# Embedding projections and two LayerNorms moved between the last two products of an MLP, with partial results combined one stage earlier

## The chip, the core and the metric

The kernel runs on one core of a Trainium2 chip. The metric is the device time of one execution in microseconds (us); the time before is the median of three runs. The core has a matrix engine (TensorE, PE in the profile), a vector engine (VectorE, DVE), an engine for activations and copies (ScalarE, ACT), a general one (GpSimd, POOL) and a queue that issues DMA transfers (SyncE, SP). The engines run in parallel, each through its own instructions in a fixed order, and wait for each other by semaphores.

## The reference, cut to what matters

Two layers over 512 tokens with a width of 1024. The token mixers (an mLSTM in layer 0, windowed attention in layer 1) are not touched by the change. The end of each layer is:

```python
for i in range(DEPTH):                      # 2 layers
    ...                                     # token mixer -> mix
    x = layer_norm(DEEPNORM_ALPHA * x + mix, mix_ln_g[i], mix_ln_b[i])
    x = layer_norm(DEEPNORM_ALPHA * x + squared_relu_mlp(x, mlp_w_up[i], mlp_w_down[i]), mlp_ln_g[i], mlp_ln_b[i])
    x = x + jax.nn.sigmoid(x @ ple_w_gate[i] + ple_b_gate[i]) * (p[i] @ ple_w_proj[i])

def squared_relu_mlp(x, w_up, w_down):      # 1024 -> 4096 -> 1024
    return jnp.square(jax.nn.relu(x @ w_up)) @ w_down
```

`p[i]` is the per-layer embedding, 512 x 256. The product `p[i] @ ple_w_proj[i]` needs nothing of x; the gate product `x @ ple_w_gate[i]` needs the x of the second LayerNorm.

## The kernel before, in words

All products run in float32 split into a high and a low part: `split` lets ACT cast the raw tile (L76, 128x1024) to the high part and DVE subtract it (L77) for the low part, and `mm3` issues three matmuls (high-high, high-low, low-high: L88, L89, L90). Weights arrive through SP's queue in a ring of three `raw` buffers and are split into rings of six `whi` and six `wlo` buffers; a DMA waits until its raw buffer has been split, a cast until the products that read its `whi` buffer are done.

The residual stream x lies in four tiles `res[0..3]` of 128 tokens x 1024. For the products it is transposed on PE (`transpose_in`, L129, eight 128x128 blocks for a tile, in two PSUM banks of the tag `tp`, of which there are three) and written to XH by ACT (L133) and to XL by DVE (L134).

`mlp` handles the 4096 hidden columns in four quarters q. Each quarter has an up-projection (eight weight tiles, `wstat`, with relu, square and the operand sums of a Strassen-like scheme in `evac`) and then a down-projection by seven products instead of eight, called in `seven`: A11 (step M1), A12 (M2), S1 (M5), S2 (M6), S4 (M3), S3 (M7), A22 (M4). Each product has 2 x 4 k-blocks x 3 = 24 matmuls of 128x512 and two results (a = 0, 1), each in a PSUM bank (tag `mm`, five banks). `on(step, a, bank)` adds a result into the residual tiles and into the gathered partial sums T1 (M1), T6 (M6) and T7 (M7), half a tile (128x512) at a time on DVE. In quarters 0 to 2 T1, T6 and T7 are only gathered; in the last quarter they are combined and added to the residual, `bn_stats` is taken of each finished half, and `ln_finish` normalises a tile: two full-tile DVE steps (L145, L146, with the power -0.5 on POOL, L138, between) and `transpose_in`. Tiles 0 and 1 are finished in step M3 or behind it, tiles 2 and 3 in step M4. S23 and S4A in the profile are the operands of S2 and S3, and of S4 and A22.

Then `ple` loads and splits the embedding (`ph`, `pl`) and the projection weights, computes the projections (2 halves x 4 tiles x 2 k-blocks x 3 = 48 matmuls of 128x512) and copies them to `pj` tiles on ACT (L684), and then computes the gate product, 2 halves x 4 tiles x 24 matmuls, each followed by bias, sigmoid, multiply and add.

The order on each engine is not the order of the code: a scheduler reorders by priority and data dependence when the kernel is built, and the order is then fixed.

Of the kernel before, what the change touches and what calls it, by code (L numbers as in the profile page):

```python
# [45 lines left out]
def yoco_kernel(ctx: ExitStack, tc: tile.TileContext, A: dict, out: bass.AP):  # L46
# [3 lines left out]
    def pool(name, bufs=1, stack=ctx, **kw):  # L50
        return stack.enter_context(tc.tile_pool(name=name, bufs=bufs, **kw))
# [19 lines left out]
    def f32(t):  # L71
        return t.bitcast(F32)
# [36 lines left out]
    def tsl(t):  # L109
        return slice(t * P, (t + 1) * P)  # L110
# [29 lines left out]
    def ln_finish(t, st, g, b, mlp_next=True):  # L140
        mv = small.tile([P, 2], F32, tag="mv", name="mv")
        V.bn_aggr(mv, st)
# [3 lines left out]
        V.scalar_tensor_tensor(res[t], res[t], rs, b, ALU.mult, ALU.add)  # L146
# [339 lines left out]

    sp = {}

    def seven(A_, wsrc, on):

        w0, w1 = wsrc(0), wsrc(1)
        r11, r21 = two((w0, 0, True)), two((w0, 2, False))
        r12, r22 = two((w1, 0, True)), two((w1, 2, True))

        def ops(raw):
            out = []
            for c in range(2):
# [56 lines left out]
    def mlp(i, side):  # L554
# [6 lines left out]
        for q in range(NQ):  # L561
# [31 lines left out]
            if q == 0:  # L593
                j0 = 4
                w = [load_w(A["w_up"][i, j], 1024) for j in range(j0)]
                ps = [mm_bank() for _ in range(j0)]
                for a in (0, 256):
                    for j in range(j0):
                        wh, wl = w[j]
                        for k in range(KD):  # L600
                            sl = slice(k * P, (k + 1) * P)
                            mm3(ps[j][:, a:a + 256], wh[:, sl], wl[:, sl], XH[:, k, a:a + 256], XL[:, k, a:a + 256], k == 0, k == KD - 1)
                        evac(ps[j], j, a, a + 256)
            for j in range(j0, 8):
                wstat(A["w_up"][i, 8 * q + j], lambda ps: evac(ps, j, 0, S))
            last = q == NQ - 1
            lo_, hi_ = slice(0, 512), slice(512, 1024)
            gb_ = []

            def gather(acc, bank):  # L610
                if q == 0:
                    ACT.copy(acc, bank)
                else:
                    V.tensor_add(acc, acc, bank)

            def on(step, a, bank):
                r0, r1 = res[a], res[2 + a]
                t1, t6, t7 = T1[:, a, :], T6[:, a, :], T7[:, a, :]
                if step == "M1":
                    gather(t1, bank)  # L620
                    if last:
                        V.tensor_add(r0[:, lo_], r0[:, lo_], t1)
                elif step == "M2":
                    V.tensor_add(r0[:, lo_], r0[:, lo_], bank)
                    if last:
                        V.bn_stats(sts[a][:, 0, :], r0[:, lo_])
                        if a == 1:
                            for x, n in ("h", "mlp_ln_g"), ("l", "mlp_ln_b"):
                                v = pm.tile([P, 4, 256], F32R, tag=f"A11{x}", name=f"A11{x}")
                                v = f32(v).rearrange("p k c -> p (k c)")  # L630
                                nc.gpsimd.dma_start(v, A[n][i].partition_broadcast(P))  # L631
                                gb_.append(v)
                elif step == "M5":
                    V.tensor_add(r1[:, hi_], r1[:, hi_], bank)
                    if last:
                        V.tensor_add(r0[:, hi_], r0[:, hi_], r1[:, hi_])
                elif step == "M6":
                    gather(t6, bank)
                    if last:
                        V.tensor_sub(t6, t6, t1)  # L640
                        V.tensor_add(r0[:, hi_], r0[:, hi_], t6)
                elif step == "M7":
                    gather(t7, bank)
                    if last:
                        V.tensor_add(t7, t7, t6)
                        V.tensor_add(r1[:, hi_], r1[:, hi_], t7)
                        V.tensor_sub(r1[:, lo_], r1[:, lo_], t7)
                        V.bn_stats(sts[2 + a][:, 1, :], r1[:, hi_])
                elif step == "M3":
                    V.tensor_add(r0[:, hi_], r0[:, hi_], bank)  # L650
                    if last:
                        V.bn_stats(sts[a][:, 1, :], r0[:, hi_])
                        ln_finish(a, sts[a], *gb_, mlp_next=False)
                elif step == "M4":
                    V.tensor_add(r1[:, lo_], r1[:, lo_], bank)
                    if last:
                        V.bn_stats(sts[2 + a][:, 0, :], r1[:, lo_])
# [3 lines left out]
            seven(sset((at(A11), at(A12))), lambda half: [A["w_down"][i, half, 4 * q + c] for c in range(4)], on)  # L661
        mctx.close()

    def ple(i, last, side):
        plctx = ExitStack()
        pp = pool(f"pp{i}", stack=plctx, side=side, reuse_waits="tile")
        ph = pp.tile([P, 2, S], F32R, name="ph")
        pl = pp.tile([P, 2, S], F32R, name="pl")
        raw = wpool.tile([P, 1024], F32, tag="raw", name="wraw", bufs=3)
        nc.sync.dma_start(raw, A["pT"][i])  # L670
        split(raw, 1024, flat(ph), flat(pl))
        bg = bcast(A["ple_b_gate"][i])
        if not last:
            bo = bcast(A["b_b_o"])
        pjs = [sp["s"].tile([P, 1024], F32, tag="rb", name="pj", bufs=6) for _ in range(NT)]
        for half in range(2):
            hs = slice(half * 512, (half + 1) * 512)
            wph, wpl = load_w(A["w_proj"][i, half], 1024)
            for t in range(NT):
                pj = mm_bank()  # L680
                for k in range(2):
                    sl = slice(k * 512, (k + 1) * 512)
                    mm3(pj, ph[:, k, tsl(t)], pl[:, k, tsl(t)], wph[:, sl], wpl[:, sl], k == 0, k == 1)
                ACT.copy(pjs[t][:, hs], pj)  # L684
        for half in range(2):
            w = [load_w(A["w_gate"][i, half, c], 1024) for c in range(4)]
            for t in range(NT):
# [22 lines left out]
        plctx.close()  # L710
# [5 lines left out]
    ple(0, False, "right")  # L716
    c7.close()
    kctx = ExitStack()
    pk = pool("pk", stack=kctx, side="right", reuse_waits="tile")
# [209 lines left out]

    c7 = seven_pools(1, "left")  # L930
    mlp(1, "left")
    ple(1, True, "left")
    c7.close()
    pctx.close()
    mctx[0].close()
# [67 lines left out]
```

## Time and profile before

| | |
|---|---|
| time, median of 3 runs | 1261.61 us (1261.51 to 1261.62) |
| the profiled execution | 1262.99 us, its span 1261.3 us |
| mean granted PE clock | 0.972 |
| PE busy | 1196.9 us (95%) |
| DVE busy | 869.6 us (69%) |
| ACT busy | 586.7 us (47%) |
| POOL busy | 147.6 us (12%) |

The profile is one execution. Rows of the timeline give start, duration, engine, line, operation, output<-input, shape, count and, in brackets, the idle time of the engine before the row with what ended it. Matmuls overlap in the pipeline, so their rate is read from start to start. The ends of the two MLPs lie at about 552 to 597 us and 1167 to 1211 us.

### The profile page before, as it was taken

Reading aid. Unit: us, or ns where it says so; the run is one execution under the profiler, and the core shown is the slowest. Engines: PE = TensorE matmul, PEld = TensorE weight load, DVE = VectorE, ACT = ScalarE, POOL = GpSimd, SP = SyncE. Lnnn points to the kernel's source line nnn. Section 1 sums busy time; section 2 is a strip of 40 time slices with the busy share of each in tenths; the row PEclk is TensorE's granted clock in tenths of the full one; section 3 lists DMA queues with packets and bytes.
Section 4 is the critical chain, followed back from the end, with each engine's and each line's share of the span. In section 5 each row is a group of like instructions: output and inputs, shape, how many; then the busy total and the mean of one; then the engine's idle time right before and its main releaser. Section 6 shows DMA issues by size and latency. Waiting matters only on the chain.

```text
span 1261.3 us, 15669 instructions
## 1 busy us (share of the span) xinstructions
PE 1196.9 (95%) x5918; PEld 1017.4 (81%) x5918; DVE 869.6 (69%) x1429; ACT 586.7 (47%) x1010; POOL 147.6 (12%) x245
## 2 busy tenths in 40 slices
PE   8999999999999999977989898999999999999598
PEld 8899988888888888865868897789888888888386
DVE  6555567696595785996474788486848759569934
ACT  4544542664553644634233545336546346364331
POOL 1011110000000000000154663210000000000100
PEclk9999999999999999996999999989999999999799
DMA  7222224506125053132242211351350521602311
GB/s 242 90 87 68 84 76 161 198 17 192 60 93 161 14 167 101 34 121 80 84 159 67 68 35 34 127 208 34 108 159 1 184 84 65 185 18 67 117 51 50
DMA packets 35708, 124.54 MB, mean 99 GB/s; under 512 B 4065, under 2 KB 4593, under 8 KB 35633
## 3 DMA queue, kind: packets, MB, share of 16 engines
q1 hardware_dynamic: 33552, 116.46, 28.8%
q0 software_dynamic: 2080, 7.09, 1.8%
q8 instruction: 46, 0.75, 0.2%
q14 instruction: 30, 0.24, 0.1%
HBM read 119.34 MB, written 4.19 MB: 98 GB/s over the span
## 4 chain that ended last, share of the span: by engine, by line
PE 84%; DVE 10%; ACT 2%; DMA 2%; issue 2%; POOL 0%; SPq 0%; DVEq 0%; ACTq 0%
PE mm L88 26%; PE mm L89 26%; PE mm L90 26%; DVE wlo L77 1%; PE tp L129 1%; DVE res L146 1%; ACT pr L838 1%; DVE res L145 1%; DVE QS L807 1%; DVE smax L824 1%; PE tp L88 1%; DVE sc L823 1%; PE tp L89 1%; PE tp L90 1%; DMA xraw<-in_xT_dram 1%
## 5 line engine op out<-in xcount | busy, mean ns | idle before, releaser
L76 ACT CAST whi<-wraw 128x1024 fp32r<-128x1024 f32 (+1 forms) x168 | 173.6, 1037 | 257.1 <-PE mm L90 117.3
L77 DVE TENSOR_TENSOR wlo<-wraw,whi 128x1024 fp32r<-128x1024 f32 (+1 forms) x152 | 184.4, 1216 | 155.3 <-ACT whi L76 154.6
L89 PE MATMUL mm<-XL,whi 128*128 128x512 f32 (+1 forms) x640 | 236.5, 370 | 0.0
L90 PE MATMUL mm<-XH,wlo 128*128 128x512 f32 (+1 forms) x640 | 236.3, 370 | 0.0
L88 PE MATMUL mm<-XH,whi 128*128 128x512 f32 (+1 forms) x640 | 235.0, 370 | 0.2 <-ACT XH L133 0.2
L88 PE MATMUL mm<-whi,XH 128*128 128x512 f32 (+2 forms) x424 | 147.7, 349 | 7.9 <-DVE kv L769 4.1
L89 PE MATMUL mm<-wlo,XH 128*128 128x512 f32 (+2 forms) x424 | 147.6, 348 | 0.0
L90 PE MATMUL mm<-whi,XL 128*128 128x512 f32 (+2 forms) x424 | 147.3, 348 | 0.0
L90 PEld LDWEIGHTS mm<-XH,wlo 128*128 128x128 f32 x640 | 121.7, 190 | 19.9
L89 PEld LDWEIGHTS mm<-XL,whi 128*128 128x128 f32 x640 | 121.7, 190 | 19.8
L88 PEld LDWEIGHTS mm<-XH,whi 128*128 128x128 f32 x640 | 120.6, 190 | 20.3 <-ACT XH L133 0.5
L76 ACT CAST whi<-rb 128x1024 fp32r<-128x1024 f32 x80 | 84.1, 1051 | 106.5 <-PE mm L89 54.4
L77 DVE TENSOR_TENSOR wlo<-rb,whi 128x1024 fp32r<-128x1024 f32 x80 | 97.4, 1222 | 38.9 <-ACT whi L76 38.9
L88 PEld LDWEIGHTS mm<-whi,XH 128*128 128x128 f32 x424 | 82.0, 193 | 15.9 <-DVE kv L769 4.5
L89 PEld LDWEIGHTS mm<-wlo,XH 128*128 128x128 f32 x424 | 82.0, 194 | 8.2 <-issue 1.5
L90 PEld LDWEIGHTS mm<-whi,XL 128*128 128x128 f32 x424 | 82.0, 194 | 6.9 <-issue 0.8
L631 POOL DMA_DIRECT2D A11h<-in_mlp_ln_g_dram x2 | 1.2, 581 | 590.6 <-PE mm L90 590.6
L129 PE MATMUL tp<-ident,res 128*128 128x128 f32 x160 | 30.2, 339 | 35.8 <-DVE res L146 32.6
L129 PEld LDWEIGHTS tp<-ident,res 128*128 128x128 f32 x160 | 23.5, 175 | 42.4 <-issue 36.7
L89 PE MATMUL mm<-wlo,S23h 128*128 128x512 f32 x128 | 50.7, 396 | 0.0
L89 PE MATMUL mm<-wlo,S4Ah 128*128 128x512 f32 x128 | 50.6, 396 | 0.0
L88 PE MATMUL mm<-whi,S23h 128*128 128x512 f32 x128 | 50.6, 395 | 0.0
(310 smaller groups left out, 2408.7 us busy)
## 6 DMA issues: line engine op xcount, KB each, us to landing
wraw<-in_w_up_dram SPq DMA_DIRECT2D x64, 512.0 KB, 3.6
rb<-in_w_down_dram SPq DMA_DIRECT2D x48, 512.0 KB, 4.4
wraw<-in_w_down_dram SPq DMA_DIRECT2D x16, 512.0 KB, 3.9
wraw<-in_w_gate_dram SPq DMA_DIRECT2D x16, 512.0 KB, 3.6
wraw<-in_w_vo_dram SPq DMA_DIRECT2D x19, 412.0 KB, 3.3
wraw<-in_w_qk_dram SPq DMA_DIRECT2D x8, 512.0 KB, 3.9
wraw<-in_w_out_dram SPq DMA_DIRECT2D x8, 512.0 KB, 3.9
wraw<-in_w_q_dram SPq DMA_DIRECT2D x8, 512.0 KB, 4.1
```

Of the source, the lines that this page charges most:

```text
L76: ACT.copy(hi, raw)
L77: eng.tensor_sub(lo, raw, f32(hi))
L88: PE.matmul(o, lh, rh, start=start, stop=False)
L89: PE.matmul(o, lh, rl, start=False, stop=False)
L90: PE.matmul(o, ll, rh, start=False, stop=stop)
L129: PE.transpose(pt[:, tsl(j)], src[:, tsl(b + j)], ident)
L145: V.scalar_tensor_tensor(res[t], res[t], mv[:, 0:1], g, ALU.subtract, ALU.mult)
L146: V.scalar_tensor_tensor(res[t], res[t], rs, b, ALU.mult, ALU.add)
L807: V.tensor_sub(QS[other, hs, tsl(t)], pv[own], f32(QS)[own, hs, tsl(t)])
L823: V.copy_predicated(cur, mk, prev)
L824: V.tensor_reduce(smax[:, :, pr], cur, AX.X, ALU.max)
L838: ACT.activation(pt_[:, par, pr, :], scs[pr][:, par, :], AF.Exp, scale=ASCALE, bias=nm[:, par, pr:pr + 1], accum_out=sm[:, par, pr:pr + 1])
```

## The change

The embedding's load, split and projections become a function `embed`, which takes its two operand tiles from the buffers of A12 (free after product A12) where it had a memory pool of its own before. `seven` gets a callback `between`, run after the weights of the last product are split and before that product: in the last quarter it runs `embed` and then `ln_finish` for tiles 0 and 1. The combination of T1, T6 and T7 of the first three quarters goes into the fourth up-projection (14 half-tile operations per layer), so that the last quarter adds only its own results: M1 is copied by ACT, M6 and M7 are read directly out of their banks.

```diff
-    def seven(A_, wsrc, on):
+    def seven(A_, wsrc, on, between=None):
...
-        product("A22", ops(r21), "M4")
+        w = ops(r21)
+        if between:
+            between()
+        product("A22", w, "M4")
...
             for j in range(j0, 8):
                 wstat(A["w_up"][i, 8 * q + j], lambda ps: evac(ps, j, 0, S))
+                if last and j == 2:
+                    for a in range(2):
+                        r0, r1 = res[a], res[2 + a]
+                        t1, t6, t7 = T1[:, a, :], T6[:, a, :], T7[:, a, :]
+                        for op, r, x in ((V.tensor_add, r0[:, lo_], t1), (V.tensor_sub, t6, t1), (V.tensor_add, r0[:, hi_], t6),
+                                         (V.tensor_add, r0[:, hi_], r1[:, hi_]), (V.tensor_add, t7, t6),
+                                         (V.tensor_add, r1[:, hi_], t7), (V.tensor_sub, r1[:, lo_], t7)):
+                            op(r, r, x)
...
                 if step == "M1":
-                    gather(t1, bank)
                     if last:
-                        V.tensor_add(r0[:, lo_], r0[:, lo_], t1)
+                        ACT.copy(t1, bank)
+                        add(r0, lo_)
+                    else:
+                        gather(t1, bank)
...
+                elif step == "M6":
                     if last:
-                        V.tensor_add(r0[:, hi_], r0[:, hi_], r1[:, hi_])
-                elif step == "M6":
-                    gather(t6, bank)
+                        V.tensor_sub(t6, bank, t1)
+                        V.tensor_add(r0[:, hi_], r0[:, hi_], t6)
+                    else:
+                        gather(t6, bank)
+                elif step == "M7":
                     if last:
-                        V.tensor_sub(t6, t6, t1)
-                        V.tensor_add(r0[:, hi_], r0[:, hi_], t6)
-                elif step == "M7":
-                    gather(t7, bank)
-                    if last:
-                        V.tensor_add(t7, t7, t6)
+                        V.tensor_add(t7, t6, bank)
                         V.tensor_add(r1[:, hi_], r1[:, hi_], t7)
                         V.tensor_sub(r1[:, lo_], r1[:, lo_], t7)
-                        V.bn_stats(sts[2 + a][:, 1, :], r1[:, hi_])
+                        stat(2 + a, 1)
+                    else:
+                        gather(t7, bank)
                 elif step == "M3":
-                    V.tensor_add(r0[:, hi_], r0[:, hi_], bank)
-                    if last:
-                        V.bn_stats(sts[a][:, 1, :], r0[:, hi_])
-                        ln_finish(a, sts[a], *gb_, mlp_next=False)
+                    add(r0, hi_)
+                    stat(a, 1)
...
+            def between():
+                embed(i, *(pm.tile([P, 4, 256], F32R, tag=f"A12{x}", name=f"A12{x}") for x in "hl"))
+                for a in range(2):
+                    ln_finish(a, sts[a], *gb_, mlp_next=False)
```

In the new order of instructions the projections' operands carry the names A12h and A12l. On PE, at the end of product S3 in layer 0, there stood:

```order
L88 MATMUL mm<-whi,S23h 128x512
L89 MATMUL mm<-wlo,S23h 128x512
L90 MATMUL mm<-whi,S23l 128x512
L88 MATMUL mm<-whi,S4Ah 128x512
L89 MATMUL mm<-wlo,S4Ah 128x512
L90 MATMUL mm<-whi,S4Al 128x512
```

and now stand:

```order
L88 MATMUL mm<-whi,S23h 128x512
L89 MATMUL mm<-wlo,S23h 128x512
L90 MATMUL mm<-whi,S23l 128x512
L88 MATMUL mm<-whi,A12h 128x512
L89 MATMUL mm<-wlo,A12h 128x512
L90 MATMUL mm<-whi,A12l 128x512
```

All 48 projection matmuls come here, and the 24 of A22 after them. On PE, at the end of A22, there stood the transposes of all four tiles (res_1745 to res_1748 are tiles 0 to 3) and then the projections:

```order
L88 MATMUL mm<-whi,S4Ah 128x512
L89 MATMUL mm<-wlo,S4Ah 128x512
L90 MATMUL mm<-whi,S4Al 128x512
L129 MATMUL tp<-ident,res_1745 128x128 x8
L129 MATMUL tp<-ident,res_1746 128x128 x8
L129 MATMUL tp<-ident,res_1747 128x128 x8
L129 MATMUL tp<-ident,res_1748 128x128 x8
L88 MATMUL mm<-whi,ph 128x512
L89 MATMUL mm<-wlo,ph 128x512
```

and now stand those of tiles 0 and 1 and, among them, the first gate matmuls:

```order
L90 MATMUL mm<-whi,S4Al 128x512
L129 MATMUL tp<-ident,res_1745 128x128 x8
L129 MATMUL tp<-ident,res_1746 128x128 x4
L88 MATMUL mm<-whi,XH 128x512
L89 MATMUL mm<-wlo,XH 128x512
L88 MATMUL mm<-whi,XH 128x512
L89 MATMUL mm<-wlo,XH 128x512
L129 MATMUL tp<-ident,res_1746 128x128 x4
L90 MATMUL mm<-whi,XL 128x512
L88 MATMUL mm<-whi,XH 128x512
```

The transposes of tiles 2 and 3 now come after the 48 gate matmuls of tiles 0 and 1 (first half). On DVE, at the LayerNorm of the first two tiles, there stood:

```order
L145 SCALAR_TENSOR_TENSOR res_1745<-res_1745,mv,A11h 128x1024
L137 TENSOR_SCALAR rs<-mv 128x1
L145 SCALAR_TENSOR_TENSOR res_1746<-res_1746,mv,A11h 128x1024
L657 BN_STATS lst<-res_1747 128x6
L77 TENSOR_TENSOR wlo<-wraw,whi 128x1024
L648 BN_STATS lst<-res_1748 128x6
L655 TENSOR_TENSOR res_1748<-res_1748,mm 128x512
L146 SCALAR_TENSOR_TENSOR res_1745<-res_1745,rs,A11l 128x1024
L77 TENSOR_TENSOR wlo<-wraw,whi 128x1024
L146 SCALAR_TENSOR_TENSOR res_1746<-res_1746,rs,A11l 128x1024
```

and now stand (L632 adds A22's results, L134 writes the low part of the transposed tiles):

```order
L145 SCALAR_TENSOR_TENSOR res_1746<-res_1746,mv,A11h 128x1024
L146 SCALAR_TENSOR_TENSOR res_1745<-res_1745,rs,A11l 128x1024
L77 TENSOR_TENSOR wlo<-wraw,whi 128x1024
L146 SCALAR_TENSOR_TENSOR res_1746<-res_1746,rs,A11l 128x1024
L632 TENSOR_TENSOR res_1747<-res_1747,mm 128x512
L77 TENSOR_TENSOR wlo<-wraw,whi 128x1024
L632 TENSOR_TENSOR res_1748<-res_1748,mm 128x512
L636 BN_STATS lst<-res_1747 128x6
L77 TENSOR_TENSOR wlo<-wraw,whi 128x1024
L134 TENSOR_TENSOR XL<-tp,XH 128x4x128 x3
```

Both A22 additions now come after the LayerNorm of tiles 0 and 1, and two weight splits stand between them and the first low part. The 14 combining operations of each layer stand, in the order that was built, among the last products of the third quarter, between weight splits of the fourth up-projection. The order of the attention stage between the two MLPs is the same but for a few exchanged rows.

More of the change, by code (lines that the diff above doesn't have):

```diff
@@ L603, in mlp @@
                         evac(ps[j], j, a, a + 256)
+            last = q == NQ - 1
+            lo_, hi_ = slice(0, 512), slice(512, 1024)
             for j in range(j0, 8):
                 wstat(A["w_up"][i, 8 * q + j], lambda ps: evac(ps, j, 0, S))
-            last = q == NQ - 1
-            lo_, hi_ = slice(0, 512), slice(512, 1024)
+                if last and j == 2:
[6 more added lines that the diff above has]
+                            op(r, r, x)
             gb_ = []
@@ L618, in on, with add, stat @@
                 t1, t6, t7 = T1[:, a, :], T6[:, a, :], T7[:, a, :]
+                def add(r, h):
+                    V.tensor_add(r[:, h], r[:, h], bank)
+                def stat(t, half):
+                    if last:
+                        V.bn_stats(sts[t][:, half, :], res[t][:, hi_ if half else lo_])
                 if step == "M1":
-                    gather(t1, bank)
                     if last:
-                        V.tensor_add(r0[:, lo_], r0[:, lo_], t1)
+                        ACT.copy(t1, bank)
+                        add(r0, lo_)
+                    else:
+                        gather(t1, bank)
@@ L623, in on @@
                 elif step == "M2":
-                    V.tensor_add(r0[:, lo_], r0[:, lo_], bank)
-                    if last:
[L626 to L634, printed above, removed]
-                    if last:
-                        V.tensor_add(r0[:, hi_], r0[:, hi_], r1[:, hi_])
-                elif step == "M6":
-                    gather(t6, bank)
-                    if last:
-                        V.tensor_sub(t6, t6, t1)
-                        V.tensor_add(r0[:, hi_], r0[:, hi_], t6)
-                elif step == "M7":
-                    gather(t7, bank)
-                    if last:
-                        V.tensor_add(t7, t7, t6)
+                    add(r0, lo_)
@@ new lines, in on @@
+                    stat(a, 0)
+                    if last and a == 1:
+                        for x, n in ("h", "mlp_ln_g"), ("l", "mlp_ln_b"):
+                            v = pm.tile([P, 4, 256], F32R, tag=f"A11{x}", name=f"A11{x}")
+                            v = f32(v).rearrange("p k c -> p (k c)")
+                            nc.gpsimd.dma_start(v, A[n][i].partition_broadcast(P))
+                            gb_.append(v)
+                elif step == "M5":
+                    add(r1, hi_)
+                    if last:
+                        add(r0, hi_)
+                elif step == "M6":
+                    if last:
+                        V.tensor_sub(t6, bank, t1)
[3 more added lines that the diff above has]
+                elif step == "M7":
+                    if last:
+                        V.tensor_add(t7, t6, bank)
@@ L646, in on @@
                         V.tensor_add(r1[:, hi_], r1[:, hi_], t7)
                         V.tensor_sub(r1[:, lo_], r1[:, lo_], t7)
-                        V.bn_stats(sts[2 + a][:, 1, :], r1[:, hi_])
+                        stat(2 + a, 1)
+                    else:
+                        gather(t7, bank)
                 elif step == "M3":
-                    V.tensor_add(r0[:, hi_], r0[:, hi_], bank)
+                    add(r0, hi_)
+                    stat(a, 1)
+                elif step == "M4":
+                    add(r1, lo_)
@@ L651, in on @@
                     if last:
-                        V.bn_stats(sts[a][:, 1, :], r0[:, hi_])
-                        ln_finish(a, sts[a], *gb_, mlp_next=False)
-                elif step == "M4":
-                    V.tensor_add(r1[:, lo_], r1[:, lo_], bank)
-                    if last:
-                        V.bn_stats(sts[2 + a][:, 0, :], r1[:, lo_])
+                        stat(2 + a, 0)
                         ln_finish(2 + a, sts[2 + a], *gb_, mlp_next=False)
+            def between():
+                embed(i, *(pm.tile([P, 4, 256], F32R, tag=f"A12{x}", name=f"A12{x}") for x in "hl"))
+                for a in range(2):
+                    ln_finish(a, sts[a], *gb_, mlp_next=False)
@@ L660, in mlp @@
             at = lambda pair: lambda k, a: tuple(p[:, k, tsl(a)] for p in pair)
-            seven(sset((at(A11), at(A12))), lambda half: [A["w_down"][i, half, 4 * q + c] for c in range(4)], on)
+            seven(sset((at(A11), at(A12))), lambda half: [A["w_down"][i, half, 4 * q + c] for c in range(4)], on,
+                  between if last else None)
         mctx.close()
[L664 to L668, printed above, removed]
+    pjs = []
@@ L669, in ple, with embed @@
+    def embed(i, ph, pl):
         raw = wpool.tile([P, 1024], F32, tag="raw", name="wraw", bufs=3)
@@ L671, in ple @@
         split(raw, 1024, flat(ph), flat(pl))
[L672 to L675, printed above, removed]
+        ph, pl = (flat(x).rearrange("p (k s) -> p k s", k=2) for x in (ph, pl))
+        pjs[:] = [sp["s"].tile([P, 1024], F32, tag="rb", name="pj", bufs=6) for _ in range(NT)]
         for half in range(2):
@@ L684, in ple @@
                 ACT.copy(pjs[t][:, hs], pj)
+    def ple(i, last):
+        bg = bcast(A["ple_b_gate"][i])
+        if not last:
+            bo = bcast(A["b_b_o"])
         for half in range(2):
@@ L715, in yoco_kernel @@
     mlp(0, "right")
-    ple(0, False, "right")
+    ple(0, False)
     c7.close()
@@ L931, in yoco_kernel @@
     mlp(1, "left")
-    ple(1, True, "left")
+    ple(1, True)
     c7.close()
```

1 line of the change is left out of this document (removed).

## Prediction

> **What bounds the kernel now.** I read the page first, then the list of waits, then TensorE's timeline where the longest wait falls, then the other queues there.
>
> ```profile
> PE 1196.9 (95%) x5918; PEld 1017.4 (81%) x5918; DVE 869.6 (69%) x1429; ACT 586.7 (47%) x1010; POOL 147.6 (12%) x245
> ...
> PE tp L129 <- DVE res L146: 32.6, 9, 10.5
> PE sc L818 <- ACT pr L838: 4.9, 5, 2.1
> ```
>
> TensorE (PE) is busy for 95% of the span, so time can only come from work taken off it or from its waits. The second group gives total us, times and the longest: 32.6 us of waiting belong to one place, transposes (L129) that wait for VectorE's (DVE) second LayerNorm step (L146); the next wait is 4.9 us. The timeline (start, us, idle before in brackets) shows it at the end of each MLP, layer 0 first:
>
> ```profile
> 560.39 0.39 PE L90 MATMUL mm<-whi,S4Al 128*128 128x512 f32 x1
> 571.19 1.94 PE L129 MATMUL tp<-ident,res 128*128 128x128 f32 x8 [10.40 <-DVE res L146]
> 573.52 2.29 PE L129 MATMUL tp<-ident,res 128*128 128x128 f32 x8 [0.39 <-DVE mv L142]
> 578.50 1.94 PE L129 MATMUL tp<-ident,res 128*128 128x128 f32 x8 [2.69 <-DVE res L146]
> 582.28 1.94 PE L129 MATMUL tp<-ident,res 128*128 128x128 f32 x8 [1.83 <-DVE res L146]
> 583.87 0.78 PE L88 MATMUL mm<-whi,ph 128*128 128x512 f32 x1
> 584.44 0.63 PE L89 MATMUL mm<-wlo,ph 128*128 128x512 f32 x1
> 584.87 0.63 PE L88 MATMUL mm<-whi,ph 128*128 128x512 f32 x1
> ...
> 596.39 0.39 PE L90 MATMUL mm<-whi,pl 128*128 128x512 f32 x1
> 596.62 0.39 PE L88 MATMUL mm<-whi,XH 128*128 128x512 f32 x1
> ...
> 1175.27 0.39 PE L90 MATMUL mm<-whi,S4Al 128*128 128x512 f32 x1
> ...
> 1211.25 0.39 PE L88 MATMUL mm<-whi,XH 128*128 128x512 f32 x1
> ```
>
> The last product ends one pitch after its last start (596.39 to 596.62 is a pitch of 0.23): 560.62. The gate product starts at 596.62. Between them lie 36.0 us: 15.3 us idle (10.40+0.39+2.69+1.83), the transposes, and the embedding projections (ph, pl) from 583.87, 12.75 us. Layer 1 has the same gap, 1211.25 − 1175.50 = 35.75 us. Columns of the next rows: length, busy time of PE, PEld, DVE, ACT, POOL, then the granted clock.
>
> ```profile
> 560.60:571.20 10.60, 0.20 (x2) 0.04 (x1) 10.60 (x18) 2.09 (x2) 3.14 (x4) 0.62 0.76 235
> 571.20:584.20 13.00, 8.00 (x33) 6.48 (x34) 12.81 (x19) 5.04 (x8) 2.90 (x2) 0.50 0.15 51
> 596.60:640.00 43.40, 43.40 (x203) 36.00 (x202) 22.48 (x29) 13.74 (x19) 5.90 (x3) 1.00 0.24 80
> ```
>
> In the gap DVE is the busy engine and the granted clock falls to 0.50; in the gate stage PE is full at 1.00 and DVE is half idle. So PE has work that DVE could hide behind, on the wrong side of the LayerNorms.
>
> **The change part by part.**
>
> *Projections between S3 and A22.* 2 halves x 4 tiles x 2 blocks x 3 = 48 matmuls per layer move ahead of A22; at the dense pitch of 0.2336 they cost 11.2 us there and leave the gap. What they need must be ready at S3's end, 555.0 in the trace.
>
> ```profile
> 490.94 0.33 SPq L670 DMA_DIRECT2D wraw<-in_pT_dram  x1
> 545.74 2.66 SPq L83 DMA_DIRECT2D wraw<-in_w_proj_dram  x2
> 549.28 1.05 ACT L76 CAST whi<-wraw 128x1024 fp32r<-128x1024 f32 x1 [3.28 <-DMA wraw<-in_w_proj_dram]
> 551.83 1.05 ACT L76 CAST whi<-wraw 128x1024 fp32r<-128x1024 f32 x1 [1.50 <-DMA wraw<-in_w_proj_dram]
> 554.19 1.22 DVE L77 TENSOR_TENSOR wlo<-wraw,whi 128x1024 fp32r<-128x1024 f32 x1
> ```
>
> The embedding itself is asked for at 490.94, 64 us early; the two weights are split by 551.5 and 555.3 and needed at 555.0 and 560.6, so no wait. In the new kernel the embedding's buffer is released after A12's product and not at 583, which lets the weights load earlier still. Its cast and split (1.05 on ACT, 1.14 on DVE) and the eight pj copies (about 0.6 each on ACT, one per 1.4 us) only change place. Cost 0.
>
> *The first two LayerNorms behind that cover.* In the new order DVE holds, from product S3's first result to the normalised tile 1, 7 half-tile adds, 4 weight splits, 4 bn_stats, small ones for 0.3 us and 4 full-tile LayerNorm steps. From start to start:
>
> ```profile
> 557.73 0.67 DVE L646 TENSOR_TENSOR res<-res,bc 128x512 f32<-128x512 f32 x1
> 558.32 0.69 DVE L647 TENSOR_TENSOR res<-res,bc 128x512 f32<-128x512 f32 x1
> 558.92 1.22 DVE L77 TENSOR_TENSOR wlo<-wraw,whi 128x1024 fp32r<-128x1024 f32 x1
> 560.06 0.68 DVE L645 TENSOR_TENSOR bc<-bc 128x512 f32<-128x512 f32 x1
> ...
> 569.76 1.28 DVE L146 SCALAR_TENSOR_TENSOR res<-res,rs,A11l 128x1024 f32<-128x1024 f32 x1
> 570.96 1.22 DVE L77 TENSOR_TENSOR wlo<-wraw,whi 128x1024 fp32r<-128x1024 f32 x1
> ```
>
> an add takes 0.60, a split 1.14, a full-tile step 1.20. That is 11 x 0.60 + 4 x 1.14 + 0.3 + 4 x 1.20 = 16.3 us from about 553.5 (behind the second projection weight's split), so tile 1 is ready at about 569.8 and tile 0 at 567.4, a split and a step earlier. A22 now ends at 560.62 + 11.2 = 571.8. The 10.4 us wait is gone with 4.4 us to spare on tile 0.
>
> *What is late next.* After A22 the order is eight transposes of tile 0, four of tile 1, four gate matmuls, the other four of tile 1. That last group needs a PSUM bank that is free only when DVE has made tile 0's low part (L134), and ahead of it DVE holds an add, a bn_stats and a split of a gate weight whose buffer A22 was reading: 0.15+0.60+0.60+1.14+0.60, with the split before it about 3.1 to 3.8 us. PE has 12 transposes and 4 matmuls meanwhile.
>
> ```profile
> 219.39 1.03 PE L129 MATMUL tp<-ident,res 128*128 128x128 f32 x8
> 225.12 0.63 PE L129 MATMUL tp<-ident,res 128*128 128x128 f32 x4 [0.85 <-DVE res L146]
> 226.86 0.63 PE L129 MATMUL tp<-ident,res 128*128 128x128 f32 x4 [1.11 <-DVE XL L134]
> 638.42 1.03 PE L129 MATMUL tp<-ident,res 128*128 128x128 f32 x8
> 643.25 0.63 PE L129 MATMUL tp<-ident,res 128*128 128x128 f32 x4 [0.15 <-DVE XL L134]
> ```
>
> Inside a stream of matmuls eight transposes take 1.03 us against 1.94 in the gap, 0.11 each. So PE has 12 x 0.11 + 4 x 0.234 = 2.25 us of work and waits 0.9 to 1.6 us. Then 44 gate matmuls (10.3 us) cover the LayerNorms of tiles 2 and 3: DVE needs about 11 us from A22's end and PE comes to them after 14.5, so 3 us are spare. Their transposes may wait 0.15 to 1.1 us, as in the rows above. I take 2.0 us of new waits per layer; bounds 0.5 and 7, the upper one if that cover fails by about 4 us.
>
> *Partial results.* 14 half-tile adds per layer, 14 x 0.60 = 8.4 us of DVE, join the fourth up-projection, and 8 (4.8 us) leave the last quarter, where two banks are now read directly and M1 is copied by ACT. The new ones stand in DVE's queue late in the third quarter's products:
>
> ```profile
> 466.38 1.23 DVE L77 TENSOR_TENSOR wlo<-wraw,whi 128x1024 fp32r<-128x1024 f32 x1 [1.84 <-ACT whi L76]
> 471.97 1.23 DVE L77 TENSOR_TENSOR wlo<-wraw,whi 128x1024 fp32r<-128x1024 f32 x1 [1.80 <-ACT whi L76]
> 484.25 1.22 DVE L77 TENSOR_TENSOR wlo<-wraw,whi 128x1024 fp32r<-128x1024 f32 x1 [3.70 <-ACT whi L76]
> ```
>
> DVE waits 1.8 to 3.7 us before a split every 5.5 us there. Two or three adds fit into each hole, so I cost them at 0; without that cover they would be worth up to 8.4 us per layer.
>
> *Sum.* The gap shrinks to 32 transposes at 0.11 = 3.5 us plus 2.0 us of waits, and the projections' 11.2 us stand ahead of it: 36.0 − 11.2 − 3.5 − 2.0 = 19.3 us in layer 0 and 35.75 − 16.7 = 19.0 in layer 1, together 38.3. The profiled execution took 1262.99 us for a span of 1261.3, 1.4 us above the median of the three runs; 1261.61 − 38.3 = 1223.3, and I say 1223.5.
>
> **The rivals.**
>
> *A. DVE's queue takes the place of the wait.* The splits of gate weights stand between LayerNorm steps in an in-order queue, and two of them wait for buffers that the projections release. For it: DVE has no idle time in the gap's rows before (10.60 of 10.60, 12.81 of 13.00). Against it: 16.3 us of work in the 18.3 from 553.5 to 571.8. If it runs 5 us late behind its spare time, in both layers, 10 us are lost: about 1233.5. Chance 0.15.
>
> *B. The transposes stay slow.* At 1.94 us for eight, 0.24 each, 32 of them cost 32 x 0.13 = 4.3 us more, and some eight matmuls behind them 0.2 more each (584.44 to 584.87 is a pitch of 0.43): 5.9 per layer, about 1235. Against it stand the rows of 1.03 us, one of them (225.12) even behind a wait of 0.85; for it, that none of those stretches has 12 transposes and a wait together. The Trainium skill ("TensorE: Matmul & The Clock Gate", Part 4: PE-mode transpose) says that the full clock does not engage for transposes because they do not count as activity. By that rule this rival would be the likely one; the rows of 1.03 us, half the 1.94 of the gap, do not agree with it. Chance 0.12.
>
> *C. Slower.* A22 now stands behind the projections in PE's queue. If the second projection weight is split late, PE stands still with A22, its two results and the last two LayerNorms behind it. It is 5.3 us early in the trace; only a split later than 560.6 + 19 = 580 in both layers turns the sign, four or five turns of landing, cast and split (3.3 + 1.05 + 1.14 us from the rows). 6 us later than that in each layer gives 1261.6 + 12 = 1273.6. Chance 0.03.
>
> *D. No gain.* The order could have put the projections elsewhere; it does not, so this needs waits that give all of it back: 1261, chance 0.02.
>
> **How the numbers follow.** My forecast has 0.68, the rivals 0.15, 0.12, 0.03 and 0.02. With waits of 0.5 us per layer the sum gives 1220.3; a little under that is the lower end, 1219. The upper end takes in A and B, and the upper bound of the new waits (10 us more, 1233.5), with some room: 1238. A measurement of this kernel tells about 0.2% from no change, 2.5 us. Faster 0.95, same 0.02, slower 0.03.
>
> **What would show it.** Between S23 and the last S4A rows 48 matmuls on A12h and A12l with pj copies beside them and no idle; the wait of L129 for L146 under 4 us in total; transposes of 1.03 us; granted clock near 1.00 from the last product to the gate product; the stretch from A22's end to the 48th gate matmul about 14.5 us (16 transposes, 1.6 us of waits, 48 x 0.234). Wrong would be a long wait of the first transpose for L146 (A), a clock of 0.5 beside transposes of 1.94 (B), an idle PE ahead of the first A12h matmul (C), or new idle time in the fourth up-projection, which would mean that its adds delay splits.

## The result, and the profile after

The changed kernel takes 1222.96 us (median of 4 runs, 1220.87 to 1223.72) against 1261.61 before: a ratio of 0.9691 (95% interval 0.9674 to 0.9708), 38.65 us less. The profiled execution took 1223.72 us, its span is 1222.0 us and its mean granted clock 0.991.

The page and the list of waits of the new kernel (total us, times, the longest):

```profile
PE 1185.8 (97%) x5918; PEld 1007.5 (82%) x5918; DVE 877.2 (72%) x1445; ACT 586.6 (48%) x1014; POOL 148.1 (12%) x245
...
PE mm L88 <- DVE kv L796: 4.1, 1, 4.1
PE tp L129 <- DVE XL L134: 3.4, 4, 1.1
...
PE tp L129 <- DVE res L146: 2.4, 2, 1.5
...
PE mm L88 <- ACT XH L133: 1.3, 5, 0.3
```

The 32.6 us that the transposes waited for L146 have become 2.4, and what is left of them lies elsewhere in the kernel. PE's timeline at the end of the first MLP answers to the rows of before:

```profile
556.39 0.39 PE L88 MATMUL mm<-whi,A12h 128*128 128x512 f32 x1
...
567.63 0.40 PE L88 MATMUL mm<-whi,S4Ah 128*128 128x512 f32 x1
...
573.25 1.47 PE L129 MATMUL tp<-ident,res 128*128 128x128 f32 x12
575.04 0.50 PE L88 MATMUL mm<-whi,XH 128*128 128x512 f32 x1 [0.32 <-ACT XH L133]
575.38 0.40 PE L89 MATMUL mm<-wlo,XH 128*128 128x512 f32 x1
576.01 0.50 PE L88 MATMUL mm<-whi,XH 128*128 128x512 f32 x1 [0.24 <-ACT XH L133]
...
577.34 0.66 PE L129 MATMUL tp<-ident,res 128*128 128x128 f32 x4 [0.59 <-DVE XL L134]
...
587.85 1.47 PE L129 MATMUL tp<-ident,res 128*128 128x128 f32 x12
...
589.85 0.66 PE L129 MATMUL tp<-ident,res 128*128 128x128 f32 x4
```

S3 ends at 556.39, the projections run to 567.63 (11.24 us, no idle), A22 to 573.25, and the first transposes start with no wait. Layer 1 repeats this with the same waits (0.32, 0.24, 0.59). The rows of DVE (start, us, idle before) show why:

```profile
567.11 1.28 DVE L146 SCALAR_TENSOR_TENSOR res<-res,rs,A11l 128x1024 f32<-128x1024 f32 x1
569.39 1.23 DVE L77 TENSOR_TENSOR wlo<-wraw,whi 128x1024 fp32r<-128x1024 f32 x1 [1.00 <-ACT whi L76]
570.53 1.28 DVE L146 SCALAR_TENSOR_TENSOR res<-res,rs,A11l 128x1024 f32<-128x1024 f32 x1
571.73 0.68 DVE L632 TENSOR_TENSOR res<-res,mm 128x512 f32<-128x512 f32 x1
573.13 1.22 DVE L77 TENSOR_TENSOR wlo<-wraw,whi 128x1024 fp32r<-128x1024 f32 x1 [0.72 <-ACT whi L76]
574.27 0.68 DVE L632 TENSOR_TENSOR res<-res,mm 128x512 f32<-128x512 f32 x1
```

Tile 0 is normalised at 568.4, 4.9 us before A22 ends, and tile 1 at 571.8, 2.3 us before its transposes can start. Three windows (length, busy us of PE, PEld, DVE, ACT, POOL, then the granted clock) show the same stretch: the projections, the first transposes, and the gate product of tiles 0 and 1.

```profile
553.50:565.70 12.20, 12.20 (x53) 9.81 (x53) 11.95 (x19) 6.48 (x9) 2.51 (x3) 1.00 0.71 236
571.30:575.00 3.70, 3.42 (x22) 2.73 (x20) 2.98 (x5) 2.60 (x4) 0.00 (x0) 1.00 0.62 144
575.00:586.00 11.00, 10.13 (x44) 7.85 (x45) 10.31 (x16) 2.18 (x4) 2.70 (x2) 1.00 0.29 97
```

DVE is still nearly full, but PE is full beside it, and the clock that fell to 0.50 before stays at 1.00.

The two spans are compared between landmarks on PE (each stretch starts where the one above it ends): the start of the first A11 product of a layer's MLP, of its fourth quarter's, the end of S3 in that quarter, the first matmul behind the kv add (start of layer 1's attention), and the last wait of the program (the last gate group, for `xr`).

| stretch, us | before | after | difference |
|---|---|---|---|
| start to layer 0's first A11 | 272.53 | 273.91 | +1.38 |
| to the fourth quarter's A11 (holds the 14 early adds) | 248.74 | 248.74 | 0 |
| to S3's end | 33.74 | 33.74 | 0 |
| S3's end to the kv add | 104.53 | 85.27 | −19.26 |
| kv add to layer 1's first A11 | 229.25 | 226.71 | −2.54 |
| to S3's end | 281.15 | 281.15 | 0 |
| S3's end to the last gate group | 82.95 | 64.11 | −18.84 |
| rest | 8.4 | 8.4 | 0 |

They sum to 39.3 us, the difference of the two spans (1261.3 and 1222.0).

### The profile page after: what moved, and what is told of

It is laid out like the page before. It is cut to its first block, busy times and chain, and to the rows that moved or that the text cites. A ratio compares the mean times of both kernels' runs of the same rounds, so it can differ in the third digit from the quotient of the medians.

```text
span 1222.0 us, 15691 instructions
## 1 busy us (share of the span) xinstructions
PE 1185.8 (97%) x5918; PEld 1007.5 (82%) x5918; DVE 877.2 (72%) x1445; ACT 586.6 (48%) x1014; POOL 148.1 (12%) x245
## 4 chain that ended last, share of the span: by engine, by line
PE 84%; DVE 7%; issue 3%; ACT 3%; DMA 2%; POOL 1%; SPq 0%; DVEq 0%; ACTq 0%; POOLq 0%
PE mm L88 26%; PE mm L90 26%; PE mm L89 26%; DVE wlo L77 1%; ACT pr L865 1%; DMA xraw<-in_xT_dram 1%; ACT whi L76 1%; PE tp L129 1%; DVE QS L834 1%; DVE smax L851 1%; PE tp L88 1%; DVE sc L850 1%; PE tp L89 1%; PE tp L90 1%; POOL wlo L77 1%
## 5 line engine op out<-in xcount | busy, mean ns | idle before, releaser
L89 PEld LDWEIGHTS mm<-XL,whi 128*128 128x128 f32 x640 | 121.2, 189 | 19.6
L88 PE MATMUL mm<-whi,S4Ah 128*128 128x512 f32 x128 | 50.6, 395 | 0.0
L90 PE MATMUL mm<-whi,S4Al 128*128 128x512 f32 x128 | 50.3, 395 | 0.0
```

Of the source, the lines that this page charges most:

```text
L88: PE.matmul(o, lh, rh, start=start, stop=False)
L89: PE.matmul(o, lh, rl, start=False, stop=False)
L90: PE.matmul(o, ll, rh, start=False, stop=stop)
```

## Experiments

Medians are given, with the range of the runs, and behind them the ratio to the kernel before with its 95% interval; the kernel before, run beside each group, had 1261.18, 1262.29 and 1260.95 us. "T0" is the first transpose after the last product.

**One part without the other.** The first kernel is the changed one with the combining put back into the last quarter:

```diff
-                if last and j == 2:
-                    for a in range(2):
...
-                            op(r, r, x)
...
                 if step == "M1":
+                    gather(t1, bank)
                     if last:
-                        ACT.copy(t1, bank)
-                        add(r0, lo_)
-                    else:
-                        gather(t1, bank)
+                        V.tensor_add(r0[:, lo_], r0[:, lo_], t1)
...
```

> The changed kernel without one part: T1, T6 and T7 of the first three quarters are combined in the last quarter, as before, and not in the fourth up-projection; the projections and the first two LayerNorms stay between S3 and A22. Theory (the projections and the LayerNorms behind them make the gain; the early combining only relieves DVE): DVE has 8 half-tile adds of 0.60 us more (4.8 us) in the last quarter of each layer and 14 fewer in the fourth up-projection. Between S3 and the transposes DVE had 4.9 us to spare on tile 0 and 2.3 us on tile 1, so 0 to 3 us per layer come back as waits of the transposes for L146: 1223 to 1229 us. Rival 1 (the early combining is what makes the move possible): tile 0 and tile 1 each arrive about 5 us late and the clock falls behind that wait, 5 to 8 us per layer: 1233 to 1239 us. Rival 2 (14 adds in the fourth up-projection cost time there): up to 1 us per layer faster than the changed kernel, 1221 us or less.

Measured: 1236.2 us (1231.95 to 1236.7), 0.9789 (0.9762 to 0.9817), some 13 us more than the changed kernel. The theory was wrong on size; the first rival came out. PE and DVE of this kernel in layer 0:

```profile
575.34 1.06 PE L129 MATMUL tp<-ident,res 128*128 128x128 f32 x8 [3.98 <-DVE res L146]
...
571.59 0.68 DVE L624 TENSOR_TENSOR res<-res,mm 128x512 f32<-128x512 f32 x1
572.18 1.22 DVE L77 TENSOR_TENSOR wlo<-wraw,whi 128x1024 fp32r<-128x1024 f32 x1
573.32 0.68 DVE L624 TENSOR_TENSOR res<-res,mm 128x512 f32<-128x512 f32 x1
573.92 1.27 DVE L146 SCALAR_TENSOR_TENSOR res<-res,rs,A11l 128x1024 f32<-128x1024 f32 x1
```

The first L146 starts 19.6 us after S3's end (554.33), where in the changed kernel it starts after 10.7: 8.9 us later. The added work is only 3.6 us of that, 6 half-tile adds per layer and not the 8 of the expectation: DVE has 1429 instructions for 1445, so 28 have gone and 12 have come back. The rest is order. Added up from the trace between S3's end and that L146, adds take 4.0 us more than in the changed kernel, splits 2.4 (two more), a further bn_stats 0.6, and there is a wait of 1.8 us for the cast of a weight. Both additions of A22's results (L624, 0.60 each) are among them; in the changed kernel these additions and the wait for a cast stand behind tile 0's L146. So the early combining, whose cost was forecast as 0, is also what keeps the LayerNorms ahead of A22's results.

The second kernel has only that part. The projections get back their own pool and their place behind A22, and the first two LayerNorms go back to M3:

```diff
                 elif step == "M3":
                     add(r0, hi_)
                     stat(a, 1)
+                    if last:
+                        ln_finish(a, sts[a], *gb_, mlp_next=False)
...
-                  between if last else None)
+                  None)
...
-    def ple(i, last):
+    def ple(i, last, side):
+        plctx = ExitStack()
+        pp = pool(f"pp{i}", stack=plctx, side=side, reuse_waits="tile")
+        embed(i, pp.tile([P, 2, S], F32R, name="ph"), pp.tile([P, 2, S], F32R, name="pl"))
```

> The changed kernel with only the other part: the early combining in the fourth up-projection stays, the projections go back behind A22 with a pool of their own, and the first two LayerNorms go back to step M3 of the last quarter. Theory: the gap after A22 is bound by DVE, and shortens only by the adds that left DVE's queue there: 4 to 8 half-tile adds of 0.60, 2.4 to 4.8 us per layer, so 1252 to 1257 us. The rest of the 38.6 us, about 15 us per layer, belongs to the place of the projections. Rival (the two parts gain about half each): 1240 to 1245 us. Rival (the adds cost in the up-projection what they save at the end): 1261 us.

Measured: 1252.5 us (1251.75 to 1256.14), 0.9935 (0.9913 to 0.9958); the theory's range held. S3's end to the kv add is 100.60 us (3.9 less than before), and in layer 1 S3's end to the last gate group 79.08 (3.9 less). The waits stay, in new places: 12.7 us in eight waits for L146, and 5.1 us ahead of tile 2's transposes in each layer (this row names rs, which stands right behind tile 2's L146 in DVE's queue).

```profile
PE tp L129 <- DVE res L146: 12.7, 8, 3.0
PE tp L129 <- DVE rs L137: 10.2, 2, 5.1
```

Between these landmarks the place of the projections alone (the kernel without the early combining) gains 12.2 + 13.4 = 25.6 us, the combining alone 7.8, both 38.1: 4.7 us come only when both are there.

**Work or clock.** The kernel before, with dummy matmuls in its 10.4 us wait:

```diff
+    def filler(n):
+        ps = mm_bank()
+        t = sp["S1"][0]
+        for i in range(n):
+            PE.matmul(ps, t[:, 0, :P], t[:, 0:2, :].rearrange("p a b -> p (a b)"), start=True, stop=True)
...
+            if last:
+                filler(40)
```

> The kernel before, with 40 matmuls of 128x512 added behind product A22 of the last quarter of each layer, in the 10.4 us in which PE waits for the first LayerNorm; their result is not used. They take 40 x 0.234 = 9.4 us of that wait and move no DVE work. It parts the two gains of the change: DVE work hidden behind matmuls, and a PE clock that does not fall. Theory (DVE's chain is what is paid for, the clock is a small part): the transposes start at the same time, tile 3's arrives with DVE as before, and only its transposes (1.94 to 1.03 us) and the first matmuls of the projections (12.75 us to about 11.3) get faster: 2 to 3 us per layer, 1255.5 to 1258 us. Rival 1 (the fallen clock is much of the gap): the gap loses 5 us or more per layer, 1251 us or less. Rival 2 (matmuls cost where they stand, the wait is not free): 9.4 us per layer more, 1280 us.

Measured: 1262.89 us (1258.98 to 1264.98), 1.0012 (0.9997 to 1.0027): nothing gained and nothing lost. All three numbers missed.

```profile
572.53 1.06 PE L129 MATMUL tp<-ident,res 128*128 128x128 f32 x8 [1.32 <-DVE res L146]
574.86 2.29 PE L129 MATMUL tp<-ident,res 128*128 128x128 f32 x8 [1.27 <-DVE mv L142]
579.84 1.94 PE L129 MATMUL tp<-ident,res 128*128 128x128 f32 x8 [2.69 <-DVE res L146]
583.62 1.94 PE L129 MATMUL tp<-ident,res 128*128 128x128 f32 x8 [1.83 <-DVE res L146]
...
574.50:588.00 13.50, 8.53 (x31) 6.83 (x32) 12.05 (x19) 4.46 (x7) 2.90 (x2) 0.51 0.23 76
```

Tile 0's transposes run at the full clock (1.06 us for 1.94) and start where they did, 16.2 us after S3's end; then the clock falls again, just ahead of tile 1's transposes, and stays down through the waits of tiles 2 and 3 (0.51 in the window). The projections start 28.85 us after S3's end as before (28.86). So the gap of before was DVE's chain; matmuls in its first wait could neither shorten it nor keep the clock up behind it. The clock by itself was measured on the kernel without the early combining, where a single long wait, of 4 us, is left. Sixteen dummy matmuls fill it:

```diff
         product("A22", w, "M4")
+        if between:
+            filler(16)
```

> The kernel without the early combining, with 16 matmuls of 128x512 (3.75 us, result not used) behind product A22 of the last quarter, in the 4.0 us wait of the first transposes for L146. DVE's work is the same, so the transposes start as late as without them; what differs is that PE does not stand still. Theory (the clock falls a few us after PE stands still, to 0.50 for about 7 us, and this is what came on top of the two waits of 4 us): the clock stays at 1.00, 2 to 3 us in layer 0 and 1 to 1.5 us in layer 1 come back, 1231 to 1233.5 us against 1236.2 without them. Rival 1 (the clock follows something else): it falls as without them, 1235 to 1237 us. Rival 2 (the fill delays the transposes): 1237 us or more.

Measured: 1228.88 us (1227.6 to 1232.57), 0.9748 (0.9731 to 0.9765), below the theory's 1231 to 1233.5. The window without the fill, then a row and the window with it:

```profile
576.00:590.00 14.00, 13.15 (x51) 10.19 (x50) 11.98 (x19) 2.88 (x5) 2.71 (x2) 0.76 0.14 47
```

```profile
574.84 1.06 PE L129 MATMUL tp<-ident,res 128*128 128x128 f32 x8 [0.34 <-DVE res L146]
...
575.50:589.50 14.00, 12.79 (x62) 10.02 (x61) 12.14 (x19) 2.88 (x5) 2.71 (x2) 1.00 0.15 48
```

T0 starts 21.0 us after S3's end in both, so DVE's lateness is the same; the clock is 1.00 where it was 0.76. The stretch from S3's end to the kv add is 2.9 us shorter and that to the last gate group in layer 1 1.5 us, both as the theory said. Of what the missing combining costs in the two ends (12.5 us), 8.1 are DVE's lateness and 4.4 the clock behind it. The median fell by 7.3 us, more than 4.4: the attention stage of the profiled runs was also shorter (225.1 against 229.3 us), where the fill adds nothing. The time by itself is therefore no measure of the clock's share; the two stretches are. Why the attention stage varies is told below.

**How near the edge is.** Full-tile steps were added on DVE ahead of the first two LayerNorms, first three, then eight in each layer:

```diff
+                for _ in range(3):
+                    V.scalar_tensor_tensor(gb_[0], res[1], 0.0, gb_[0], ALU.mult, ALU.add)
                 for a in range(2):
                     ln_finish(a, sts[a], *gb_, mlp_next=False)
```

> The changed kernel with three more full-tile steps on DVE in each layer (3 x 1.20 = 3.6 us, gamma = res1 * 0 + gamma, a result that changes nothing) ahead of the LayerNorms of tiles 0 and 1. Measured spare time of DVE there: 4.9 us on tile 0, 2.3 us on tile 1. Theory 1 (only the added work counts): tile 0 stays hidden, tile 1 comes 1.3 us late, 1225 to 1227 us. Theory 2 (what counts is the whole queue: with DVE late the two additions of A22's results, a bn_stats and one or two weight splits are placed ahead of tile 0's L146, some 4 us more, as without the early combining): the first transposes wait about 3 us per layer and the clock falls behind it, 4 to 6 us per layer, 1231 to 1235 us. Rival (DVE has room for all of it): 1223 us.

Measured: 1232.42 us (1230.03 to 1237.09), 0.9773 (0.9752 to 0.9794): theory 2. T0 of this kernel:

```profile
577.24 1.10 PE L129 MATMUL tp<-ident,res 128*128 128x128 f32 x8 [3.97 <-DVE res L146]
```

The three steps take 3.4 us, less than the 4.9 us that tile 0 had to spare, and give a wait of 4.0 us, because other work moves ahead of L146 here too: both additions of A22's results (1.2 us), two splits (2.4), a bn_stats (0.6) and a wait for a cast (1.2).

> The changed kernel with eight more full-tile steps on DVE per layer (9.6 us) in the place where three were added before. With three the first transposes waited 4.0 us. Theory (DVE's queue is an in-order chain with no cover left: from there each added us is a us of PE's waiting, and the clock falls behind it): five more steps, 6.0 us, give a wait of 10 us per layer, and the transposes and first gate matmuls run at half the clock, some 3 to 4 us more: 1222 + 2 x 13 = 1248 us, 1245 to 1252 us. Rival (part of it still finds room beside the projections and A22): 1240 us or less.

Measured: 1246.97 us (1245.56 to 1249.08), 0.9891 (0.9875 to 0.9906), inside the theory's range. T0 and the clock behind it:

```profile
582.85 2.80 PE L129 MATMUL tp<-ident,res 128*128 128x128 f32 x12 [11.91 <-DVE mv L142]
...
584.00:585.00 1.00, 1.00 (x6) 1.00 (x5) 1.00 (x3) 0.73 (x2) 0.74 (x1) 0.50 0.00 0
585.00:586.00 1.00, 1.00 (x6) 0.71 (x4) 1.00 (x3) 0.73 (x2) 1.00 (x2) 0.70 0.00 0
586.00:587.00 1.00, 0.82 (x3) 0.30 (x2) 1.00 (x2) 0.27 (x1) 0.95 (x1) 1.00 0.00 0
```

(This row names mv L142, the small step right behind tile 0's L146 in DVE's queue.) Five more steps (6.0 us) turn a wait of 3.97 into 11.91 us, 7.9 more: one further split and one further bn_stats (1.9 us) have also moved ahead of L146. The two ends grow by 5.8 us (S3's end to the kv add) and 6.7 us (to the last gate group in layer 1), so beyond the edge 6 us of DVE cost about 6 us of PE.

**Towards a faster one.** The wait for L134 that is left (0.59 us) is DVE's queue: two gate-weight splits stand ahead of it. They go to POOL:

```diff
-            w = [load_w(A["w_gate"][i, half, c], 1024) for c in range(4)]
+            w = [load_w(A["w_gate"][i, half, c], 1024, GP if half == 1 and c < 2 else V) for c in range(4)]
```

> The changed kernel, with the low parts of the first two gate weights of each layer (half 1) subtracted on POOL in place of DVE, so that two splits of 1.14 us leave DVE's queue between the first LayerNorms and the first low part of the transposed tiles. Theory (the new wait of 0.59 us for L134 and the 0.32 and 0.24 for L133 are DVE's queue): the wait for L134 goes, 0.6 to 1 us per layer, 1221 to 1222.5 us. Rival (POOL takes about 2.75 us for such a split, so the products on the low weight wait for it instead): the same or up to 3 us per layer slower, 1223 to 1229 us.

Measured: 1220.61 us (1219.57 to 1223.01), 0.968 (0.9659 to 0.97). The wait is gone:

```profile
577.21 0.60 PE L129 MATMUL tp<-ident,res 128*128 128x128 f32 x4
```

and S3's end to tile 2's transposes is 30.64 us for 31.46. The changed kernel and this variant were then run beside each other:

> The changed kernel once more, beside the others on one chip, for its scatter and its clock. By its four earlier runs 1221 to 1224 us. If the 2.4 us that the attention stage lost on the kernel before (229.3 to 226.7 us from its first product behind the kv add to the second layer's first down-projection) are a matter of when the granted clock falls, and not of the order of instructions, that stage comes out anywhere between 226 and 230 us here too.

> The variant with the two splits on POOL, beside the changed kernel itself on one chip. Theory: its wait for L134 is gone (0.59 us per layer) and the stretch from the first projection matmul to tile 2's transposes is 0.8 us shorter, so 1.2 to 1.6 us faster than the changed kernel, 1220 to 1222 us. Rival: no difference beyond the scatter of 2 to 3 us.

Measured: 1221.87 us (1221.16 to 1223.43) and 1221.02 (1219.94 to 1223.66), ratios 0.9687 (0.9673 to 0.97) and 0.9681 (0.9666 to 0.9697). The 0.8 us per layer are seen in the trace, but the runs do not tell the two kernels apart. The attention stage took 226.4 us in this execution of the changed kernel; in the two of the variant it took 226.1 and 227.8, with one order of instructions.

The longest single wait left in this part is the kv add at the start of layer 1's attention, which both kernels have. It waits for a bias, kvb. Its DMA, and that of the bias bq, stand on POOL's queue behind 40 memsets; now they stand ahead:

```diff
+    kvb = pk.tile([P, 512], F32, name="kvb")
+    nc.gpsimd.dma_start(kvb, A["kv_b"].partition_broadcast(P))
...
     for t in range(NT):
         for vv in (vph[t], vpl[t]):
             for j in range(KVH + 1):
                 GP.memset(f32(vv)[:, 2 * HD * j:2 * HD * j + HD], 0.0)
-    kvb = pk.tile([P, 512], F32, name="kvb")
-    nc.gpsimd.dma_start(kvb, A["kv_b"].partition_broadcast(P))
...
```

> The variant with two splits on POOL, and one more edit at another place: at the start of the second layer's attention the DMAs of two biases (kvb, bq) are issued on POOL's queue ahead of 40 memsets and not behind them. In the changed kernel PE waits there 4.1 us (5.1 in the variant) for the kv add, which waits for kvb: issued at 636.3, landed 5.3 us later; the memsets before it take 3.5 us. Theory (the landing of kvb sets the end of that wait): it is issued 3.0 to 3.5 us earlier, the wait falls to 1 to 2 us, and the clock, which falls to 0.50 behind that wait for some 6 us, stays up if the wait is under 3 us: 3 to 6 us less than 1221.0, 1215 to 1218 us. Rival 1 (the DMA waits for memory that the gate stage frees late, so an earlier place in the queue changes nothing): 1221 us. Rival 2 (the memsets, later by 1 us, delay the v operands): 1222 us or more.

Measured: 1217.52 us (1215.47 to 1223.89), 0.9661 (0.9636 to 0.9687). POOL's queue in the changed kernel, and in this one with its wait:

```profile
636.45 0.60 POOL L757 DMA_DIRECT2D kvb<-in_kv_b_dram  x1
```

```profile
631.28 0.60 POOL L753 DMA_DIRECT2D kvb<-in_kv_b_dram  x1
...
PE mm L88 <- DVE kv L796: 2.2, 1, 2.2
```

The two executions start at different times: counted from S3's end in layer 0, kvb is issued after 80.1 us in the changed kernel and after 75.8 here, and it lands 4.3 and 5.9 us later. Its landing still ends the wait, as the theory said. The wait fell to 2.2 us, a little over the 1 to 2 expected. That the clock stays up behind a wait under 3 us did not come true: it falls, for 3.4 us where it was 6.8. The median is the lowest of the study, 4.4 us below the changed kernel's in its second series, on another chip and with overlapping intervals, so the runs alone do not show a gain.

## Why the prediction was right

The sum forecast 19.3 us less at the end of layer 0 and 19.0 at that of layer 1; the traces show 19.26 and 18.84. That the medians agree to 0.5 us as well (1223.5 forecast, 1222.96 measured) is partly luck: the four runs lie 2.9 us apart, and stretches that the change leaves alone moved by +1.38 and −2.54. Point by point:

- *Projections ahead of A22, 11.2 us:* 11.24 and 11.15, with no idle before their first matmul; the weights were not late (rival C).
- *LayerNorms behind that cover:* forecast for tiles 0 and 1, moved by the 1.4 us by which this execution was later: 568.8 and 571.2. Measured 568.4 and 571.8. The instruction-by-instruction sum of DVE's queue was the step that carried the forecast. Its counts were exact (7 adds, 4 splits, 4 bn_stats, 4 full-tile steps), but it left out two waits for casts (0.25 and 1.00 us), and the queue started 0.8 us earlier than assumed; the two partly cancel.
- *Transposes at 0.11 us:* twelve take 1.47 us (0.12 each), four 0.41 to the next matmul. Rival B is out. (The row of 225.12 in its paragraph is four transposes in 0.63 us, not eight in 1.03.) The Trainium skill ("TensorE: Matmul & The Clock Gate", Part 4: PE-mode transpose) says that the full clock does not engage for transposes, which do not count in the same way as PE being busy. The first half does not agree with these runs: the row of 573.25 runs at a granted clock of 1.00. Nor does the second where eight steps were added: the clock rose at about 585.6, 2.8 us after the wait, and of those PE had spent 2.4 us on transposes and 0.3 on a matmul.
- *Tiles 2 and 3:* DVE was to need about 11 us behind A22's end and PE to come to them after 14.5. Measured 11.5 and 14.6, with no wait.
- *New waits, 2.0 us per layer taken:* 0.32 + 0.24 + 0.59 = 1.15. This term was 0.85 too large; what made up for it is that a matmul next to transposes or a wait takes longer to the next start than 0.23, 0.31 to 0.34 right behind one and 0.39 to 0.40 right ahead of one, which is about 1 us for eight of them.
- *Early combining at no cost:* 248.74 us for the three quarters that hold it, before and after. Of the last quarter 6 adds left in each layer and not 8: DVE has 1445 instructions for 1429. The step priced only the cost. Without it the same move is worth 13 us less, and alone it is worth 8.7; the sum had that gain in it unnamed, in the short DVE queue.
- *Rival A:* its chance was fair, its point was not. It began at 5 us beyond the spare time; three steps of 1.20, less than the spare time of tile 0, already cost 10 us in the runs. The margin of 4.4 us was counted as time that more work could use, and it holds only as long as the order stays.
- *Not forecast:* +1.38 at the start and −2.54 in the attention stage. They are scatter. The start of the same code varies from 271.0 to 274.5 us over the profiled runs; why is open. The attention stage took 229.3 us in the kernel before, and 230.1, 226.6 and 226.1 in three kernels with exactly its order on PE there (the fill of 40, the combining alone, the splits on POOL). It goes with the clock: over the twelve profiles it takes 225.1 to 228.1 us where the clock is at half for 12.5 to 16.1 us of it, and 229.3 to 230.1 where it is for 18.7 to 19.7. Before and after differ in this at the end of the output product:

```profile
835.00:856.00 21.00, 18.37 (x128) 17.77 (x127) 14.84 (x22) 11.75 (x21) 1.45 (x1) 0.84 0.59 226
```

```profile
815.00:836.00 21.00, 18.38 (x142) 17.35 (x141) 17.46 (x26) 14.22 (x25) 2.91 (x2) 1.00 0.56 226
```

The waits ahead of it are the same (1.5 and 1.1 us); what differs is where they lie in time. Within one execution all changes of the granted clock lie on a grid of 3.413 us: in the kernel before it falls at 563.13, rises at 587.03 and falls at 658.71, 7 and 21 steps apart, and the twelve profiles all agree, each with a phase of its own. Here, in the kernel before, PE was busy for 1.58 us of the step from 836.20 to 839.62, and the clock fell; in the changed kernel it was busy for 1.81 us of the step from 818.22 to 821.63, and the clock did not fall. The Trainium skill ("TensorE: Matmul & The Clock Gate", Part 1, What's actually happening) tells of an activity window that runs freely, by its figure 3.4 us long; these traces agree with it.

## What to carry to other kernels

When an engine waits at the end of a stage, look for work of its own that needs nothing of the late result and sits on the wrong side of it; then add up the other engine's whole queue, instruction by instruction in the built order, to see whether it fits behind that cover. Spare time in an in-order queue is not a budget: a little more work can change what stands ahead of the one instruction that matters, so shorten that queue too. Dummy work in a wait can keep the clock up. Here it gained where no other long wait followed (16 matmuls in a 4 us wait) and gained nothing where three more did (40 in a 10.4 us wait).

## What the runs showed of the hardware

- The granted clock falls after the last matmul's end with a delay that differs: 2.4 us in the kernel before (560.8 to 563.1), 3.1 at the kv add of the changed kernel, 4.4 with eight added steps, 5.3 without the early combining. The grid of 3.413 us accounts for this. Without the early combining both layers have the same wait of 4.0 us ahead of the first transposes; in layer 0 the clock falls 5.3 us after the last matmul and eight transposes take 1.06 us, in layer 1 it falls after 3.4 us and they take 1.94:

```profile
1177.99 1.94 PE L129 MATMUL tp<-ident,res 128*128 128x128 f32 x8 [4.03 <-DVE res L146]
```

- How long PE is busy within a step of the grid tells more than the length of one wait. Added up over the twelve profiles, the full clock fell behind every step in which PE was busy for less than 1.5 us and behind none with more than 2.0; it came back only behind steps with 2.7 us or more. So it also fell with no wait over 1.32 us: with the fill of 40, the step from 571.35 to 574.76 held 1.07 us of transposes between two waits.
- A split of 128x1024 takes 2.4 us on POOL in the gate stage where DVE needs 1.14. No matmul waited for one there.
